# The trailing query product of each attention score taken over all 128 rows instead of 64

## The chip, the cores and the metric

The kernel runs on one core of one Trainium2 chip. The metric is the device time of one execution in microseconds (us); the median of three executions stands for the kernel.

## What is computed

Two layers over 1024 tokens of width 1024, in float32: an RMSNorm, one input projection, three mixers side by side (pooling, spatial gate, attention), an output projection onto the residual stream, then a second RMSNorm and a squared-ReLU MLP of width 4096. The change touches the attention, which has 8 heads of width 64 and no softmax: the weight of a key is its own sigmoid times the product of what all keys between it and the query left over.

```python
def stick_breaking_attention(q, k, v):
    ...
        z = jnp.einsum('bhqd,bhkd->bhqk', qi, k).astype(jnp.float32) * inv_sqrt_d
        ...
        log_beta = jax.nn.log_sigmoid(z)
        log_1m = jnp.where(causal, jax.nn.log_sigmoid(-z), 0.0)
        after = lax.cumsum(log_1m, axis=3, reverse=True) - log_1m
        a = jnp.where(causal, jnp.exp(log_beta + after), 0.0)
        return jnp.einsum('bhqk,bhkd->bhqd', a.astype(v.dtype), v)
```

## The kernel before

Features lie on the 128 partitions and tokens, in reversed order, on the free axis, in two chunks c of 512. Every large product runs as three single-pass products of operands that are split exactly into a leading and a trailing part of type float32r (`mm3`, L187 to L197). The tiles `xh`, `xl`, `wh`, `wl` are such parts of x and of a weight tile, and `pj` is the PSUM bank of an input projection.

A layer's attention goes through four head pairs `pr`, and each pair through 8 units: four pairs of query blocks (`c`, `j`) for each head `h` of the pair. A unit calls `sticks` twice, once per query block, and then `attend` of the unit before it (L527 to L537). Between units stand steps of projections: values, the next pair's k and q, pooling and gate (`fill`, L514 to L525). The last head pair has the first projections of the other mixers between its units.

`sticks` (L344) makes the score `z` of 128 queries with up to 512 keys in two products that accumulate into one bank:

- L354 multiplies `qh` by `kx`. A `kx` tile holds the leading part of one head's keys on 64 partitions and the trailing part on the other 64; a `qh` tile holds the leading part of q twice. One product over 128 rows therefore gives q-leading times all of k.
- L355 multiplies `ql`, the trailing part of q, by the leading part of k, over the 64 rows `HI[h]` alone (partitions 0 to 63 for head 0, 64 to 127 for head 1).

Then ScalarE makes two sigmoids `s` and `a` of z (L359, L360), GpSimd masks the diagonal block (L363), VectorE scans `s` to running products (L370), and GpSimd multiplies (L368, L373). `attend` transposes the weights `a` on TensorE (L391), ScalarE and VectorE split them into `th` and `tl` (L395, L397), TensorE multiplies both by the values into the one bank `av` (L401, L402), and L407 and L408 take that bank out to `y`.

`q_evac` (L316) makes `qh` and `ql` from a finished projection. Both heads of a pair share one `ql` tile of which each fills 64 rows; there are two such tiles, one per token chunk. ScalarE writes `qh` (L322), GpSimd its copy (L323), and VectorE `ql` (L326).

The order of the instructions is not written out by hand: the Tile framework traces the program and its scheduler orders each engine's queue by a timeline of its own (`schedule_with_timeline_sim`), helped by priorities (`early`) for the splits and evacuations. Each queue then runs strictly in the order given.

`add_sq` (L122) sums squares for the RMSNorm. At the very start, where x comes from memory, two engines keep a sum each: GpSimd in a tile of tag `rbc`, VectorE in a tile of tag `th`. The tag `rbc` also holds the inverse RMS laid out along the free axis (`bcast`, L160), and has three buffers.

Of the kernel before, what the change touches and what calls it, by code (L numbers as in the profile page):

```python
# [7 lines left out]
F32 = mybir.dt.float32  # L8
F32R = mybir.dt.float32r
# [16 lines left out]
NBIG = 4  # L26
# Pairs of query and key blocks of a unit, by its query blocks.
BLK = (15, 11, 7, 3)

# Units of attention are ordered by head pair, query blocks and head. Each product ahead of  # L30
# its use is traced between two units; from unit PACED on it follows their scores.
POOL_STEPS = 8
# [3 lines left out]
EVAC_EARLY = 400  # L36
# The last down projection by (chunk, first token, tokens), so that the final norm overlaps it.
TAIL = ((1, 0, 512), (0, 0, 256), (0, 256, 256))
# [8 lines left out]

# Column layout of the small constant array.
C_N1 = 0
# [7 lines left out]
def trunk_kernel(tc, xT, w_in, w_out, w_up, w_down, pool_w, sgw, sgb, sgn, cst, outT):  # L57
    """Decoder trunk with features on partitions and time, reversed, on the free axis.

    Every large product runs as three single-pass products of operands that are  # L60
    split exactly into a leading and a trailing part (float32r). The split of x
    carries the RMSNorm gain; the inverse RMS is applied to the products.
    """
    nc = tc.nc

    with ExitStack() as ctx:
# [44 lines left out]
        def put_x(k, c, src, gain):  # L111
            """Split src * gain (feature tile k, token chunk c) into xh + xl."""
            g = cs[:, gain + k : gain + k + 1]
            h = t512("xh", 16, F32R)
            nc.scalar.activation(h, src, AF.Copy, scale=g)
            lo = t512("xl", 16, F32R)
            nc.vector.scalar_tensor_tensor(
                out=lo, in0=src, scalar=g, in1=h.bitcast(F32), op0=ALU.mult, op1=ALU.subtract
            )
            xh[k, c], xl[k, c] = h, lo  # L120

        def add_sq(k, c, src, two=None):  # L122
            """Add the squares of src; two: a pool for a second sum, kept by another engine."""
            if k == 0:
                acc[c] = []
            new = len(acc[c]) <= int(two is not None)
            if new:
                acc[c].append(t512("th", 2, F32, two) if acc[c] else t512("rbc", 3))
            a = acc[c][k % len(acc[c])]
            sq = a if new else tmp()  # L130
            if two is None or k % 2:
                nc.scalar.activation(sq, src, AF.Square)
            else:
                nc.gpsimd.tensor_mul(sq, src, src)
            if not new:
                (nc.vector if two is not None and k % 2 else nc.gpsimd).tensor_add(a, a, sq)

        def rms_col(c):
            """Inverse RMS of chunk c, per token on partitions: rst[c][:, block]."""
            rst[c] = inv_rms([[a[:, b * P : (b + 1) * P] for a in acc[c]] for b in range(4)])  # L140
# [15 lines left out]
        def rms_row(c):  # L156
            """The same along the free axis, on all partitions: rbc[c]."""
            rbc[c] = bcast(rst[c], 4)

        def bcast(r, n):  # L160
            pb = psm()
            for b in range(n):
                nc.tensor.matmul(pb[:, b * P : (b + 1) * P], r[:, b : b + 1].broadcast_to([P, P]), ident, start=True, stop=True)
            bc = t512("rbc", 3)
            nc.scalar.copy(bc[:, 0 : n * P], pb[:, 0 : n * P])
            return bc
# [7 lines left out]
        def load_w(src, pool=None, tag="w", bufs=2):  # L174
            """Load a [128, 1024] weight tile and split it."""
            raw = per.tile([P, D], F32, tag="raw", name=nm("raw"), bufs=2)
# [10 lines left out]
        def mm3(ps, wx, first, last):  # L187
            """Accumulate the three products of each ((wh, wl), (xh, xl)) pair into ps."""
            n = len(wx)
# [9 lines left out]
        def proj(w, c, bank=None):  # L199
            """[128 features, 512 tokens] of x @ W for one column tile of W."""  # L200
            ps = (bank or psj)()
            mm3(
                ps,
                [((w[0][:, k * P : (k + 1) * P], w[1][:, k * P : (k + 1) * P]), (xh[k, c], xl[k, c])) for k in range(KT)],
                True, True,
            )
            return ps

        def proj_tok(w2, c, o, out):
            """[128 tokens, 256 features] of x @ W; w2 holds two halves of the rows of W."""  # L210
            for k in range(KT):
# [4 lines left out]
        def tok_steps(w2, start, evac):  # L216
            """One step per token block; two blocks share a bank."""
            bank = []
# [33 lines left out]
        def next_w(ahead=True):  # L252
            """The next weight tile in the order of use; ahead: also start on the one after it."""
            if not ready:
# [9 lines left out]
        for l in range(DEPTH):  # L264
# [3 lines left out]

# [1 line left out]
            arp = tc.tile_pool(name=f"ar{l}", bufs=1, side="right", reuse_waits="tile")  # L270
            ar = arp.__enter__()

            with (
# [8 lines left out]
                def v_steps(hf):  # L282
                    """Steps of the value projection of head pairs 2 hf and 2 hf + 1."""
                    w2 = []
# [31 lines left out]
                def q_evac(pr, c, ps):  # L316
                    t = tmp()
                    nc.vector.tensor_mul(t, ps, rbc[c])
                    qlo = t512("ql", 2, F32R, at)
                    for h in range(2):  # L320
# [3 lines left out]
                            out=qt[LO[h]], in0=t[HI[h]], scalar1=1.0, scalar2=0.0, op0=ALU.mult, op1=ALU.add  # L324
                        )
                        nc.vector.tensor_sub(qlo[HI[h]], t[HI[h]], qt[HI[h]].bitcast(F32))  # L326
                        qh[pr, h, c] = qt
                    ql[pr, c] = qlo

# [14 lines left out]
                def sticks(pr, h, i):  # L344
                    """Attention weights of query block i: {chunk of keys: [128 queries, 512 keys]}."""
                    c, o = divmod(i, 4)
                    qs = slice(o * P, (o + 1) * P)
                    prev, res = None, {}
                    for kc in ((0, 1) if c == 0 else (1,)):
# [4 lines left out]
                        nc.tensor.matmul(z[:, 0:w], qh[pr, h, c][:, qs], kt[:, lo:CH], start=True, stop=False)  # L354
                        mm = nc.tensor.matmul(z[:, 0:w], ql[pr, c][HI[h], qs], kt[HI[h], lo:CH], start=False, stop=True)  # L355
                        last_qk[0] = mm.ins.name
# [21 lines left out]
                def attend(pr, c, j, h, aw):  # L378
                    """Attention output of head h of a pair for query blocks 2 j and 2 j + 1."""
                    po = ap.tile([P, CH], F32, tag="av", name=nm("av"), bufs=1)  # L380
# [68 lines left out]
                def spread(steps, lo, hi):  # L449
                    """Trace the steps after the sticks of units lo to hi - 1, by their cost."""  # L450
                    cost = [BLK[units[n][2]] for n in range(lo, hi)]
# [17 lines left out]
                def pool_steps():  # L469
                    """Projection of the pooling mixer; its tiles take the place of used values."""  # L470
                    w = []
# [68 lines left out]

# [1 line left out]
            pop = tc.tile_pool(name=f"po{l}", bufs=1, space=PSUM, reuse_waits="tile")  # L542
# [54 lines left out]
            with tc.tile_pool(name=f"mx{l}", bufs=1, reuse_waits="tile") as mx:  # L597
# [3 lines left out]

                # pooling mixer
                pw = tmp()[:, 0:256].rearrange("p (i d) -> p i d", i=2)
# [43 lines left out]

                # spatial gate
                sw = tmp().rearrange("p (h t) -> p h t", h=4)
# [14 lines left out]
                def gelu(dst, src, t):  # L664
                    """dst = gelu(src), tanh form; src in SBUF."""
                    nc.gpsimd.tensor_mul(t, src, src)
# [51 lines left out]

                # output projection: the attention half of the width, then the rest
                split_y(1)  # L720
# [17 lines left out]

# [1 line left out]
            misc[0] = psg  # L740

            def finish(c, t, n, parts):
                """The final norm of tokens t to t + n - 1 of chunk c."""
                nb = n // P
# [72 lines left out]
def _layout(i):  # L817
# [7 lines left out]
    def mtiles(w):  # L825
        # [L, rows, cols] -> [L, cols/128, 128, rows]: one tile per 128 columns
        r, c = w.shape[1:]
        return w.reshape(L, r // P, P, c // P, P).transpose(0, 3, 2, 1, 4).reshape(L, c // P, P, r)

    def vtiles(w):  # L830
        # [L, 1024, cols] -> [L, cols/256 * 2, 128, 4 * 256]
        c = w.shape[2]
# [49 lines left out]
```

## Time and profile before

| | us |
|---|---|
| median of three executions | 2382.85 |
| lowest and highest | 2380.62, 2382.92 |
| span of the profiled execution | 2380.7 |
| granted TensorE clock, mean over that span | 0.983 |

The page gives the profiled execution's span alone. The three executions lie between 0.1 us under that span and 2.2 us over it, so next to nothing lies around it. The attention of the first layer lies in the first fifth of the span, from about 41 to 368 us, and that of the second from about 1222 to 1535 us. PE is the TensorE's matmuls and PEld its weight loads, which run beside them; DVE is VectorE, ACT ScalarE, POOL GpSimd. A row of a timeline starts with the instruction's start, then its duration. Matmuls are pipelined, so each row of a matmul overlaps the next one, and what a matmul occupies of the engine is the distance from its start to the start of the next.

### The profile page before, as it was taken

To read this page: it belongs to the slowest core of one execution; us is meant where nothing else is said; L and a number is where in the kernel's file an instruction comes from. 1 tells how busy PE (TensorE), PEld (TensorE's weight loads), DVE (VectorE), ACT (ScalarE), POOL (GpSimd) and SP (SyncE) were. 2 spreads that over 40 slices of the span, in tenths; PEclk is the share of its full clock that TensorE was granted. 3 is DMA by queue.
4 is the path that set the end of the run, shared out by engine and by line. 5 is a ranking of instruction groups with operands and counts; after the bars stand their busy time and mean duration, and the time that the engine had idled before them with its cause. 6 is when DMAs were issued, how large, how long until landed. Compare 5 with 4: busy or idle time off the path is not lost.

```text
span 2380.7 us, 28532 instructions
## 1 busy us (share of the span) xinstructions
PE 2333.8 (98%) x11224; PEld 1924.1 (81%) x11224; DVE 1264.0 (53%) x1606; ACT 728.8 (31%) x1321; POOL 803.3 (34%) x857
## 2 busy tenths in 40 slices
PE   8999999999999999999999999999999999999997
PEld 6887787788888888888887887878888888888887
DVE  7777668853432342342558777697433433432334
ACT  5556453430120120120445655534210210120121
POOL 6567575430110110110346757464110110110115
PEclk8999999999999999999999998999999999999998
DMA  3000102221220220220301010131211210220211
GB/s 125 27 28 28 33 10 89 67 62 31 67 62 18 62 71 9 62 71 18 120 23 36 19 40 28 32 98 45 71 35 37 71 45 30 68 62 18 62 36 71
DMA packets 40246, 118.40 MB, mean 50 GB/s; under 512 B 5040, under 2 KB 7600, under 8 KB 40112
## 3 DMA queue, kind: packets, MB, share of 16 engines
q1 hardware_dynamic: 38448, 114.48, 15.6%
q8 instruction: 88, 1.44, 0.3%
q10 hardware_dynamic: 1664, 2.10, 0.2%
q14 instruction: 46, 0.38, 0.0%
HBM read 108.17 MB, written 8.39 MB: 49 GB/s over the span
## 4 chain that ended last, share of the span: by engine, by line
PE 88%; DVE 6%; issue 3%; POOL 2%; ACT 1%; DMA 0%; DVEq 0%; SPq 0%; POOLq 0%; ACTq 0%
PE pj L191 14%; PE pj L196 14%; PE pj L197 14%; PE po L197 11%; PE po L196 11%; PE po L191 11%; PE z L355 3%; PE t L391 2%; PE z L354 2%; PE av L402 2%; PE av L401 1%; DVE s L370 1%; DVE yl L109 1%; DVE kx L691 1%; DVE xh L758 1%
## 5 line engine op out<-in xcount | busy, mean ns | idle before, releaser
L779 POOL TENSOR_TENSOR tmp<-tmp 128x512 f32<-128x512 f32 x128 | 177.6, 1387 | 1125.2 <-ACT ah L778 1118.0
L191 PE MATMUL pj<-xh,wh 128*128 128x512 f32 x1344 | 527.5, 392 | 0.0
L197 PE MATMUL pj<-xh,wl 128*128 128x512 f32 x1344 | 525.5, 391 | 0.0
L196 PE MATMUL pj<-xl,wh 128*128 128x512 f32 x1344 | 525.0, 391 | 0.0
L191 PE MATMUL po<-ah,dh 128*128 128x512 f32 (+1 forms) x1056 | 402.3, 383 | 2.3 <-DVE xa L798 2.3
L197 PE MATMUL po<-ah,dl 128*128 128x512 f32 (+1 forms) x1056 | 402.4, 384 | 0.0
L196 PE MATMUL po<-al,dh 128*128 128x512 f32 (+1 forms) x1056 | 402.2, 383 | 0.0
L798 DVE TENSOR_TENSOR xa<-po,xa 128x512 f32<-128x512 f32 (+1 forms) x264 | 177.9, 675 | 413.3 <-PE po L197 413.1
L778 ACT ACTIVATE ah<-tmp 128x512 fp32r<-128x512 f32 x128 | 80.4, 628 | 727.1 <-DVE tmp L774 727.1
L191 PEld LDWEIGHTS pj<-xh,wh 128*128 128x128 f32 x1344 | 252.4, 188 | 54.4 <-issue 3.2
L197 PEld LDWEIGHTS pj<-xh,wl 128*128 128x128 f32 x1344 | 252.3, 188 | 53.4 <-issue 1.7
L196 PEld LDWEIGHTS pj<-xl,wh 128*128 128x128 f32 x1344 | 252.5, 188 | 52.9 <-issue 1.6
L191 PEld LDWEIGHTS po<-ah,dh 128*128 128x128 f32 x1056 | 199.2, 189 | 41.2 <-DVE xa L798 2.5
L373 POOL TENSOR_TENSOR a<-a,s 128x255 f32<-128x255 f32 (+1 forms) x192 | 223.4, 1166 | 26.0 <-DVE s L370 13.6
L196 PEld LDWEIGHTS po<-al,dh 128*128 128x128 f32 x1056 | 199.3, 189 | 38.8
L197 PEld LDWEIGHTS po<-ah,dl 128*128 128x128 f32 x1056 | 199.2, 189 | 38.7
L774 DVE SCALAR_TENSOR_TENSOR tmp<-pj,rbc 128x512 f32<-128x512 f32 x124 | 85.5, 690 | 206.4 <-PE pj L197 196.5
L108 ACT CAST wh<-raw 128x1024 fp32r<-128x1024 f32 x116 | 121.6, 1048 | 198.9 <-PE pj L196 139.5
L109 DVE TENSOR_TENSOR wl<-raw,wh 128x1024 fp32r<-128x1024 f32 x116 | 154.5, 1332 | 33.8 <-ACT wh L108 32.9
L781 DVE TENSOR_TENSOR al<-tmp,ah 128x512 fp32r<-128x512 f32 x128 | 90.1, 705 | 146.2 <-POOL tmp L779 146.2
L370 DVE TENSOR_TENSOR_SCAN s<-s 128x256 f32<-128x256 f32 (+3 forms) x128 | 128.8, 1012 | 44.2 <-POOL s L363 41.7
L108 ACT CAST dh<-raw 128x1024 fp32r<-128x1024 f32 x64 | 67.2, 1049 | 207.7 <-DMA raw<-in_w_down 207.7
(165 smaller groups left out, 3552.0 us busy)
## 6 DMA issues: line engine op xcount, KB each, us to landing
raw<-in_w_up SPq DMA_DIRECT2D x64, 512.0 KB, 3.6
raw<-in_w_down SPq DMA_DIRECT2D x64, 512.0 KB, 3.6
raw<-in_w_in SPq DMA_DIRECT2D x36, 512.0 KB, 3.6
raw<-in_w_out SPq DMA_DIRECT2D x16, 512.0 KB, 3.6
tmp<-in_xT SPq DMA_DIRECT2D x16, 256.0 KB, 2.7
xd<-xa SPq DMA_DIRECT2D x16, 256.0 KB, 2.0
tmp<-xd SPq DMA_DIRECT2D x16, 256.0 KB, 2.7
a<-in_xT SPq DMA_DIRECT2D x12, 256.0 KB, 5.3
```

Of the source, the lines that this page charges most:

```text
L108: nc.scalar.copy(hi, src)
L109: nc.vector.tensor_sub(lo, src, hi.bitcast(F32))
L191: mm = nc.tensor.matmul(ps, ah, bh, start=first and i == 0, stop=False)
L196: nc.tensor.matmul(ps, ah, bl, start=False, stop=False)
L197: nc.tensor.matmul(ps, al, bh, start=False, stop=last and i == n - 1)
L370: nc.vector.tensor_tensor_scan(sl, sl, sl, 1.0 if prev is None else prev[:, CH - 1 : CH], ALU.mult, ALU.bypass)
L373: nc.gpsimd.tensor_mul(a[:, lo + 1 : CH], a[:, lo + 1 : CH], s[:, lo : CH - 1])
L774: nc.vector.scalar_tensor_tensor(out=r, in0=ps, scalar=0.0, in1=rbc[c], op0=ALU.max, op1=ALU.mult)
L778: nc.scalar.activation(h, r, AF.Square)
L779: nc.gpsimd.tensor_mul(r, r, r)
L781: nc.vector.tensor_sub(lo, r, h.bitcast(F32))
L798: nc.vector.tensor_add(x, ps, x)
```

## The change

L355 runs over all 128 rows. For that each head gets a `ql` tile of its own (tags `ql0`, `ql1`, two buffers each), whose 64 rows `LO[h]` GpSimd sets to zero each time a tile is made: 32 new instructions, four for each head pair and layer. The zero rows meet the trailing part of k, so the score stays the same. To make room the tag `rbc` loses one of its three buffers, and the GpSimd sum at the start moves from an `rbc` tile to a tile of tag `tl` in the attention's pool. Comments are taken out too, which moves later lines by two.

```diff
         def add_sq(k, c, src, two=None):
...
-                acc[c].append(t512("th", 2, F32, two) if acc[c] else t512("rbc", 3))
+                acc[c].append(t512("rbc", 2) if two is None else t512("th" if acc[c] else "tl", 2, F32, two))
...
-            bc = t512("rbc", 3)
+            bc = t512("rbc", 2)
...
                 def q_evac(pr, c, ps):
                     t = tmp()
                     nc.vector.tensor_mul(t, ps, rbc[c])
-                    qlo = t512("ql", 2, F32R, at)
                     for h in range(2):
                         qt = t512("qh", 4, F32R, at)
                         nc.scalar.copy(qt[HI[h]], t[HI[h]])
...
+                        qlo = t512(f"ql{h}", 2, F32R, at)
+                        nc.gpsimd.memset(qlo[LO[h]].bitcast(F32), 0.0)
                         nc.vector.tensor_sub(qlo[HI[h]], t[HI[h]], qt[HI[h]].bitcast(F32))
-                        qh[pr, h, c] = qt
-                    ql[pr, c] = qlo
+                        qh[pr, h, c], ql[pr, h, c] = qt, qlo
...
-                        mm = nc.tensor.matmul(z[:, 0:w], ql[pr, c][HI[h], qs], kt[HI[h], lo:CH], start=False, stop=True)
+                        mm = nc.tensor.matmul(z[:, 0:w], ql[pr, h, c][:, qs], kt[:, lo:CH], start=False, stop=True)
```

No instruction but the 32 memsets is added or taken away on any compute engine. The scheduler however makes a somewhat different order of the same work in the attention of both layers. Two places follow; the numbers in the names are the program's own and differ between the two kernels.

VectorE, first layer, where the last head pair begins (`s` are scans, `tl` the trailing parts of the transposed weights, `pa` the pooling projection). Before:

```order
L326 TENSOR_TENSOR ql_3093<-tmp_3091,qh_3098 64x512
L370 SCALAR_TENSOR_TENSOR s_2991<-s_2991 128x384
L370 SCALAR_TENSOR_TENSOR s_3138<-s_3138 128x256
L370 SCALAR_TENSOR_TENSOR s_3004<-s_3004,s_2991 128x512
L397 TENSOR_TENSOR tl_2855<-t_2848,th_2853 128x512
L397 TENSOR_TENSOR tl_3018<-t_3012,th_3016 128x384
```

The same place in the changed kernel:

```order
L481 TENSOR_TENSOR pa_3132<-pj_3133,rbc_269 128x512
L372 SCALAR_TENSOR_TENSOR s_3012<-s_3012 128x384
L372 SCALAR_TENSOR_TENSOR s_3162<-s_3162 128x256
L399 TENSOR_TENSOR tl_2873<-t_2866,th_2871 128x512
L372 SCALAR_TENSOR_TENSOR s_3025<-s_3025,s_3012 128x512
L399 TENSOR_TENSOR tl_3039<-t_3033,th_3037 128x384
```

The 512-wide `tl` has moved ahead of the 512-wide scan that stood before it; the order of TensorE's rows around it is the same in both.

GpSimd, a little earlier in the same layer, in the last units of the third head pair (`a` and `s` are the attention weights and sticks, `qh` the copy of q for the fourth pair, the memset of `tmp` belongs to the pooling mixer). Before:

```order
L363 AFFINE_SELECT s_2802<-s_2802 128x128
L373 TENSOR_TENSOR a_2793<-a_2793,s_2792 128x511
L604 MEMSET tmp_4139 128x256
L323 TENSOR_SCALAR qh_3094<-tmp_3091 64x512
L651 AFFINE_SELECT tmp_4207<-tmp_4207 128x512
L363 AFFINE_SELECT a_2803<-a_2803 128x128
L373 TENSOR_TENSOR a_2803<-a_2803,s_2802 128x383
```

The same place in the changed kernel:

```order
L365 AFFINE_SELECT s_2820<-s_2820 128x128
L375 TENSOR_TENSOR a_2811<-a_2811,s_2810 128x511
L328 MEMSET ql_647_3117 64x512
L365 AFFINE_SELECT a_2821<-a_2821 128x128
L375 TENSOR_TENSOR a_2821<-a_2821,s_2820 128x383
L370 TENSOR_TENSOR a_2834<-a_2834,s_2820 128x1
L375 TENSOR_TENSOR a_2834<-a_2834,s_2833 128x511
L606 MEMSET tmp_4163 128x256
```

A memset of a `ql` tile now stands between a mask and the next products, and the other mixers' preparations come later. The first four memsets of the first layer stand at the head of GpSimd's queue, behind the memset of the identity matrix and ahead of the first squares; those of the second layer stand behind the last sums of squares and ahead of the inverse RMS.

## Rows read from the trace of the kernel before

**Rows 1.** The page: busy time, share of span and instructions of each engine.

```profile
PE 2333.8 (98%) x11224; PEld 1924.1 (81%) x11224; DVE 1264.0 (53%) x1606; ACT 728.8 (31%) x1321; POOL 803.3 (34%) x857
```

**Rows 2.** The page: the chain that ended last, shares of the span by engine.

```profile
PE 88%; DVE 6%; issue 3%; POOL 2%; ACT 1%; DMA 0%; DVEq 0%; SPq 0%; POOLq 0%; ACTq 0%
```

**Rows 3.** Windows, last two head pairs, layer 0: length, busy PE, PEld, DVE, ACT, POOL, PEclk.

```profile
194.00:276.00 82.00, 80.58 (x420) 63.10 (x419) 62.09 (x79) 45.92 (x98) 50.05 (x72) 1.00 0.13 40
276.00:342.00 66.00, 60.66 (x321) 48.67 (x321) 45.94 (x57) 35.62 (x81) 47.69 (x67) 0.84 0.04 13
```

**Rows 4.** Line L355: durations in ns, and the count of each shape.

```profile
L355 PE MATMUL z<-kx,ql x192: 222/490/793, 41.2 to 1508.2; 64*128 64x512 f32 x96, 64*128 64x256 f32 x32, 64*128 64x128 f32 x32, 64*128 64x384 f32 x32
```

**Rows 5.** Timeline of PE's matmuls, 300 to 312 us: start, duration, line, rows*columns, shape.

```profile
300.74 0.28 PE L354 MATMUL z<-kx,qh 128*128 128x256 f32 x1
300.95 0.38 PE L355 MATMUL z<-kx,ql 64*128 64x256 f32 x1
301.26 0.38 PE L402 MATMUL av<-tl,v 128*128 128x256 f32 x1
...
302.90 0.50 PE L354 MATMUL z<-kx,qh 128*128 128x512 f32 x1
303.34 0.49 PE L355 MATMUL z<-kx,ql 64*128 64x512 f32 x1
303.76 0.39 PE L401 MATMUL av<-th,v 128*128 128x256 f32 x1
303.98 0.22 PE L354 MATMUL z<-kx,qh 128*128 128x128 f32 x1
304.13 0.33 PE L355 MATMUL z<-kx,ql 64*128 64x128 f32 x1
304.39 0.50 PE L354 MATMUL z<-kx,qh 128*128 128x512 f32 x1
...
305.70 0.28 PE L191 MATMUL pj<-wh,xh 128*128 128x256 f32 x1
305.82 0.29 PE L196 MATMUL pj<-wl,xh 128*128 128x256 f32 x1
```

**Rows 6.** Timeline, 150 to 175 us: another score, and ordinary 512-column products.

```profile
153.88 0.40 PE L197 MATMUL pj<-xh,wl 128*128 128x512 f32 x1
153.88 0.19 PEld L191 LDWEIGHTS pj<-xh,wh 128*128 128x128 f32 x1
...
154.11 0.39 PE L191 MATMUL pj<-xh,wh 128*128 128x512 f32 x1
...
161.12 0.40 PE L354 MATMUL z<-kx,qh 128*128 128x512 f32 x1
161.44 0.18 PEld L355 LDWEIGHTS z<-kx,ql 64*128 64x128 f32 x1 [0.25 <-issue]
161.44 0.49 PE L355 MATMUL z<-kx,ql 64*128 64x512 f32 x1
...
161.87 0.39 PE L196 MATMUL pj<-wl,xh 128*128 128x256 f32 x1
```

**Rows 7.** Timeline, 268 to 284 us: the longest wait of PE in that attention.

```profile
279.18 1.95 DVE L370 TENSOR_TENSOR_SCAN s<-s,s 128x512 f32<-128x512 f32 x1
...
281.06 1.12 DVE L397 TENSOR_TENSOR tl<-t,th 128x512 fp32r<-128x512 f32 x2
...
281.77 0.58 PE L402 MATMUL av<-tl,v 128*128 128x256 f32 x1 [2.91 <-DVE tl L397]
```

**Rows 8.** Timeline of POOL at the start.

```profile
0.78 0.21 POOL masks.py:197 MEMSET ident<- 128x128 f32 x1 [0.29 <-POOLq L872]
...
4.36 1.04 POOL L134 TENSOR_TENSOR rbc<-a 128x512 f32<-128x512 f32 x1 [3.00 <-DMA a<-in_xT]
```

**Rows 9.** Timeline of POOL at the turn of the layers.

```profile
1206.49 2.00 POOL L153 TENSOR_TENSOR rst<-rst,mhalf 128x4 f32<-128x4 f32 x2 [13.72 <-DVE rst L149]
```

**Rows 10.** Groups by shape: the copies of q on POOL.

```profile
L323 POOL TENSOR_SCALAR qh<-tmp 64x512 fp32r<-64x512 f32 x32 | 30.6, 956 | 20.7 <-DVE tmp L318 10.6 <-issue 6.6 <-PE z L354 1.5
```

## The prediction

> **What bounds the kernel now.** I read the page first, then the chain, then the windows by head pair, then the timeline of TensorE (PE) around a few scores. The page shows PE busy for 98% of the span, and no other engine above 53% [rows 1]; the chain that ended last lies on PE for 88% of its length [rows 2]. A microsecond saved on PE is therefore worth something nearly everywhere, if the others keep up. The windows tell where they might not. In the third head pair PE is busy for 80.58 of 82 us, and VectorE (DVE), the next engine, for 62.09. In the fourth PE is busy for only 60.66 of 66 us, and its mean granted clock is 0.84 [rows 3]. With two levels, 1.2 and 2.4 GHz, a mean of 0.84 over 66 us means some 21 us at 1.2 GHz. The reader should see two different stretches: in one everything waits for PE, and I take the first two head pairs to be like it; in the other PE waits for others too.
>
> **What a score costs on PE.** What counts is the distance from one matmul's start to the next. An ordinary product of 512 columns takes 153.88 to 154.11 = 0.23 us, and one of 256 columns 305.70 to 305.82 = 0.12 [rows 5, 6]. A score of 512 columns is two products. In one of them the 128-row product starts at 302.90, the 64-row one at 303.34 and the next instruction at 303.76: 0.44 + 0.42 = 0.86 us [rows 5]. In another it is 161.12, 161.44, 161.87, so 0.32 + 0.43 = 0.75 [rows 6]. Two ordinary products would take 0.46. The weight loads show why: an ordinary load starts one product ahead (the load for the product at 154.11 starts at 153.88), but the load for the 64-row product starts at 161.44, in the same instant as its product, after 0.25 us in which nothing that the profile shows held it [rows 6]. Going into the 64-row product and coming out of it, a load of about 0.19 us stands uncovered. The way in shows as 0.32 to 0.44 us and the way out as 0.42 to 0.43, instead of 0.23.
>
> **The main term: both products over 128 rows.** I take it that a 128-row product with half its weights zero runs like every other 128-row product, whose loads are covered. The saving for each score is what it takes now less two ordinary products:
> - 512 columns: 0.75 to 0.86 less 0.46 is 0.29 to 0.40; 96 of them [rows 4] give 28 to 38 us, middle 33.
> - 256 columns: 300.74 to 300.95 to 301.26 is 0.52, less 0.24 is 0.28; 32 give 9 us [rows 4, 5].
> - 384 columns: no row here; between the two above I take 0.31, 32 give 10 us (9 to 13).
> - 128 columns: 303.98, 304.13, 304.39 is 0.41; an ordinary one is no longer than one of 256 columns, so at least 0.41 less 0.24 = 0.17; 32 give 5.5 us [rows 4, 5].
>
> The sum is 58 us, with bounds of 51 and 65. The trace does not show a 128-row product with zero rows; the bound from the other side is that nothing is saved (a rival below). I take the full value, because all other 128-row products of the trace, whatever they hold, run at the ordinary distance.
>
> The Trainium skill has a rule that speaks against this term. Its page "TensorE: Matmul & The Clock Gate", section "Why this matters for your kernels", says that a single matmul over few rows takes as long as one over 128, and that the gain of few rows lies only in running several at once. Taken alone it would make the sum zero, since the columns stay the same. The trace agrees for the load itself but not for the distance between starts, 0.42 against 0.23 us [rows 5, 6].
>
> **What is given back.** The 58 us leave PE, but the chain of a score through ScalarE, GpSimd (POOL) and DVE is as long as before. The four head pairs of the two layers hold equal numbers of scores, so each of the eight takes 7.25 us of the saving.
> - Three quarters, 43.5 us: a third head pair would take 82 - 7.25 = 74.75 us, and DVE's 62.09 us would fill 83% of it, POOL's 50.05 us 67% [rows 3]. That leaves room but more collisions; I take a return of one eighth, 5 us (0 to 20).
> - The last head pair of both layers, 14.5 us: PE already idles 5.3 us of 66 there [rows 3]. A PE that comes earlier to the same waits only waits longer. I take two thirds back, 9.5 us (0 to 14.5).
> - The longest wait there, 2.91 us for DVE's `tl`, stands behind a scan of 1.95 us on DVE [rows 7]. In the new order that `tl` comes before the scan, so the wait loses up to 1.95 us, if the same happens in both layers 4 us; I take 2, as the scan feeds work that is wanted soon after.
>
> **The memsets.** 32 on POOL. Their price is not in the trace; the nearest rows are a memset of 128 columns, 0.21 us [rows 8], and POOL's copy of 64x512, 0.956 us [rows 10]. That is 7 to 31 us on an engine that is idle for two thirds of the span; nearer by shape is the copy, by kind the memset, and I take 0.7 each, 22 us. The first four lie in the 3.00 us in which POOL waits for the first x [rows 8]; the next such four in the 13.72 us before the inverse RMS of the second layer [rows 9]. The other 24 stand in the queue between masks and products of the attention. In a head pair four of them, 2.8 us (up to 3.8), raise POOL's share of the third pair's shortened 74.75 us from 67 to 71%. A memset waits for the last use of its tile by PE, and the masks of the next units are queued behind it, which the scans on DVE want. I cost it at nothing on the path, as the cover is POOL's own idle time; if that cover is gone, each costs its 0.2 to 1 us, at most 24 us in all.
>
> **The smaller buffers.** `rbc` with two buffers holds the two chunks' rows; at the turn to the MLP and at the final norm a third would be wanted only while the first is still read, and its readers are done a projection earlier. The sum moved to `tl` changes no engine. I cost both at zero.
>
> **The sum.** 2380.7 - 58 + 5 + 9.5 - 2 = 2335.2 us of span. The three executions lie 0.1 under to 2.2 over the span, so I add 1: **2336 us**, 2.0% faster. For this case alone the bounds of the saving and of the returns give 2318 to 2354.
>
> **The rivals.**
> - *The clock recovers too.* The 21 us at 1.2 GHz in the last head pair cost up to 10 us of work, in each layer [rows 3]. If the shorter waits and denser products keep the clock up, up to 20 us come on top: 2336 - 20 = 2316, and with smaller returns as little as 2300; I put it at 2312. For it: the reordered `tl`. Against it: PE comes earlier to every other wait.
> - *The attention is bound by its chains.* If DVE's and POOL's queues, contending with each other, can't run at 83% and 71%, two thirds of the saving turn into waits: 2380.7 - 19 = 2362. For it: the fourth head pair as it is now; against: PE idles 1.4 us in all of the third.
> - *The rows don't matter.* The uncovered loads come from something else, such as the two products' shared bank or operands, and stay: 2381 to 2384, no change. Against it: the projections also add product after product to one bank, at 0.23 us.
> - *Slower: waits that take the clock down.* A wait like that of 2.91 us [rows 7] ends in a stretch with 21 us at 1.2 GHz [rows 3]; if half of that belongs to it, it loses 5 us of work besides, and such an event costs about 8 us. The saving of 58 us is eaten by seven of them, and from the eighth on the kernel is slower; with nine it takes 2380.7 - 58 + 72 = 2395. For it: a fuller DVE, and a memset on POOL that waits for PE ahead of the masks. Against: the third head pair, with more projection steps between its units, keeps a granted clock of 1.00 [rows 3].
>
> **How the numbers follow.** The forecast has 0.64, the better clock 0.12, bound chains 0.13, no change 0.04, slower 0.07. Faster by over 0.2% (about what a measurement of this kernel can tell from no change) is the first three together, 0.89; within 0.2% is 0.04; slower by over 0.2% is 0.07. The range reaches over the forecast's own, over half of the better clock down to 2308 and over half of the bound chains up to 2364.
>
> **What would show it.** In the profile after, the weight load of the second score product starts ahead of its product, and the distances at both score lines are 0.23 us at 512 columns; that decides the main term. The windows of the first three head pairs are each 6 to 7 us shorter with PE still busy throughout: right for the first return. In the fourth, PE idles longer than 5.3 us and the stretch is shortened by 2 to 4 us: right for the second. New waits of PE for `tl` or for a scan's product, and a granted clock under 0.84, would make the prediction too low; a distance of 0.42 that stays would make it wrong altogether.

## The result and the profile after

The changed kernel takes **2353.2 us** (median; executions from 2352.5 to 2358.1) against 2382.75 for the kernel before in the same comparison: a recorded ratio of 0.9886, 95% interval 0.9872 to 0.9900 (the two medians by themselves give 0.9876), so 29.6 us or 1.2% faster. The forecast was 2336 us with a range of 2308 to 2364. The sign and the main mechanism were right; some 17 us of the expected gain are missing, and the runs below are about where they went.

The page of the changed kernel, engine busy times and the chain that ended last, answering to [rows 1, 2]:

```profile
PE 2268.2 (96%) x11224; PEld 1917.9 (82%) x11224; DVE 1264.1 (54%) x1606; ACT 725.5 (31%) x1321; POOL 824.4 (35%) x889
...
PE 79%; DVE 9%; POOL 6%; issue 3%; ACT 2%; DMA 0%; SPq 0%; POOLq 0%; DVEq 0%; ACTq 0%
```

PE is busy 65.6 us less, yet the span is only 28.8 us shorter (2380.7 to 2351.9). The other 37 us are new idle time of PE, and nine hundredths of the chain have passed from PE to VectorE, GpSimd and ScalarE.

The second product of the score, all shapes, answering to [rows 4], and two scores on PE at 290 us, answering to [rows 5], with the weight load that belongs to the first of the rows (start, duration, line, rows*columns, shape):

```profile
L357 PEld LDWEIGHTS z<-kx,ql x192: 186/191/338, 43.4 to 1480.6; 128*128 128x128 f32 x192
L357 PE MATMUL z<-kx,ql x192: 222/391/629, 43.5 to 1480.8; 128*128 128x512 f32 x96, 128*128 128x256 f32 x32, 128*128 128x128 f32 x32, 128*128 128x384 f32 x32
```

```profile
289.78 0.19 PEld L357 LDWEIGHTS z<-kx,ql 128*128 128x128 f32 x1
...
290.01 0.39 PE L357 MATMUL z<-kx,ql 128*128 128x512 f32 x1
...
290.24 0.28 PE L403 MATMUL av<-th,v 128*128 128x256 f32 x1
...
290.53 0.45 PE L356 MATMUL z<-kx,qh 128*128 128x512 f32 x1
290.81 0.39 PE L357 MATMUL z<-kx,ql 128*128 128x512 f32 x1
291.05 0.28 PE L191 MATMUL pj<-wh,xh 128*128 128x256 f32 x1
```

The way out of the second product is now 290.24 - 290.01 = 0.23 and 291.05 - 290.81 = 0.24 us, where it was 0.42 to 0.43; the way in is 0.28 here and 0.236 in the median of the 512-column scores, though a quarter of them still take over 0.31. The weight load takes 0.19 us as before, but it starts 0.23 us ahead of its product (289.78 to 290.01), beside other work. Before, 131 of the 192 loads of this line stood behind 33.6 us of idle time that the profile puts down to "issue"; now none does.

The first layer's four head pairs, before and after (length of the stretch, then busy us of PE, PEld, DVE, ACT and POOL with their counts, and the granted clock; [rows 3] showed two of these stretches, cut a little differently). Before:

```profile
41.20:120.00 78.80, 77.83 (x422) 63.03 (x422) 58.97 (x77) 42.89 (x97) 50.56 (x68) 0.91 0.09 28
120.00:194.60 74.60, 74.60 (x443) 61.35 (x442) 58.32 (x77) 44.08 (x98) 49.99 (x68) 1.00 0.08 22
194.60:275.70 81.10, 79.68 (x416) 62.40 (x414) 61.29 (x79) 45.02 (x96) 49.15 (x71) 1.00 0.14 41
275.70:367.70 92.00, 86.66 (x517) 73.42 (x516) 58.35 (x73) 46.51 (x100) 54.07 (x71) 0.89 0.08 24
```

After:

```profile
43.50:115.10 71.60, 66.99 (x432) 60.75 (x432) 56.95 (x73) 43.00 (x98) 48.57 (x66) 0.98 0.10 30
115.10:185.70 70.60, 66.26 (x423) 59.32 (x422) 59.66 (x80) 41.72 (x94) 51.51 (x73) 0.98 0.08 24
185.70:263.70 78.00, 74.66 (x426) 65.85 (x425) 60.85 (x79) 46.02 (x99) 52.04 (x75) 0.96 0.14 42
263.70:352.00 88.30, 77.36 (x517) 70.77 (x516) 57.81 (x72) 45.50 (x99) 56.52 (x75) 0.90 0.07 22
```

The stretches are shorter by 7.2, 4.0, 3.1 and 3.7 us, and PE's idle time in them, the length less its busy time, has gone from 1.0, 0.0, 1.4 and 5.3 us to 4.6, 4.3, 3.3 and 10.9. In the second layer they are shorter by 4.4, 1.5, 2.3 and 1.9. The first stretch owes a good part of its 7.2 to a clock that went from 0.91 to 0.98.

PE's longest waits after, by what it waited for (us in total, times, longest):

```profile
PE av L404 <- DVE tl L399: 12.5, 11, 4.1
PE t L393 <- DVE tl L399: 9.4, 5, 3.8
PE av L403 <- DVE y L410: 8.9, 8, 1.9
...
PE pj L191 <- DVE v L300: 6.6, 4, 3.9
PE z L356 <- ACT a L362: 5.6, 8, 1.9
```

Before, the first of these groups held 5.2 us in three waits, the third 3.4 in two. What PE waits for in these groups is mostly VectorE's output.

### The profile page after: what moved, and what is told of

It reads as the page before. It is cut to its first block, busy times and chain, and to the rows that moved or that the text cites. A ratio compares the mean times of both kernels' runs of the same rounds, so it can differ in the third digit from the quotient of the medians.

```text
span 2351.9 us, 28573 instructions
## 1 busy us (share of the span) xinstructions
PE 2268.2 (96%) x11224; PEld 1917.9 (82%) x11224; DVE 1264.1 (54%) x1606; ACT 725.5 (31%) x1321; POOL 824.4 (35%) x889
## 4 chain that ended last, share of the span: by engine, by line
PE 79%; DVE 9%; POOL 6%; issue 3%; ACT 2%; DMA 0%; SPq 0%; POOLq 0%; DVEq 0%; ACTq 0%
PE pj L191 13%; PE pj L196 13%; PE pj L197 13%; PE po L197 12%; PE po L196 12%; PE po L191 11%; DVE s L372 3%; POOL a L375 2%; PE t L393 2%; PE av L403 1%; PE av L404 1%; POOL s L365 1%; POOL a L365 1%; PE z L356 1%; PE z L357 1%
```

## Experiments

Times are medians; "the changed kernel" is 2353.2 us. Each edit is to the changed kernel. The kernel before, measured beside each of them, took 2379.5 to 2382.7 us, so a difference of under some 3 us between two kernels of this section says nothing.

### The same order with 64 rows

```diff
-mm = nc.tensor.matmul(z[:, 0:w], ql[pr, h, c][:, qs], kt[:, lo:CH], start=False, stop=True)
+mm = nc.tensor.matmul(z[:, 0:w], ql[pr, h, c][HI[h], qs], kt[HI[h], lo:CH], start=False, stop=True)
```

The scheduler gives every engine the same order, row for row, so this pair differs in the rows of 192 products alone.

> The changed kernel with its second score product back on 64 rows; tiles, memsets and the order of every engine's queue are those of the changed kernel, row for row. Theory A (the saving of about 60 us on TensorE is real, and half of it comes back because TensorE reaches the ends of VectorE's and GpSimd's chains earlier): the waits of TensorE fall to about 13 us in the attention as before, the distances return to 0.42 us, and the time is that of the kernel before, 2378 to 2386 us. Theory B (half comes back because the new order and the memsets cost some 30 us by themselves, whatever TensorE does): 2353 + 60 = 2405 to 2415 us.

Measured: 2376.45 us, ratio to before 0.9977 (0.9967 to 0.9987). So tiles, memsets and new order together are worth 6 us even with the old product, and the rows alone are worth 2376.45 - 2353.2 = 23.2 us. Both layers' attention, with 64 rows and then with 128:

```profile
43.70:362.70 319.00, 311.40 (x1793) 255.29 (x1793) 237.21 (x301) 178.22 (x387) 205.81 (x285) 0.97 0.10 28
1216.90:1529.70 312.80, 305.30 (x1737) 248.78 (x1737) 230.31 (x296) 174.17 (x380) 205.06 (x283) 0.97 0.10 28
```

```profile
43.50:352.10 308.60, 285.37 (x1793) 256.78 (x1793) 235.37 (x301) 176.24 (x387) 208.63 (x286) 0.95 0.10 29
1206.10:1508.70 302.60, 279.05 (x1738) 250.89 (x1737) 229.38 (x297) 172.65 (x380) 210.42 (x283) 0.95 0.10 29
```

The attention is 20.6 us shorter in sum. PE's idle time in it rises from 15.1 to 46.8 us, 31.7 more. The mean clock falls from 0.97 to 0.95: of 632 us that is a loss of some 19 us, of 611 us one of some 31, so 12 more. The last digit of the clock makes this uncertain by some 6 us; PE's busy time in the stretches with a granted clock of 1.2 GHz, 32 us with 64 rows and 52 with 128, gives 10. So 20.6 + 31.7 + 10 to 12 = 62 to 64 us is the gross saving on PE, an estimate, of which two thirds came back as waits and as time at 1.2 GHz. VectorE's work is the same in both.

One place shows how. It is the start of the first layer's last head pair, that of [rows 7]. With 64 rows:

```profile
272.83 0.94 POOL L322 TENSOR_SCALAR qh<-tmp 64x512 fp32r<-64x512 f32 x1
...
274.42 0.29 POOL L365 TENSOR_SCALAR_AFFINE_SELECT s<-s 128x128 f32<-128x128 f32 x1
...
274.74 1.83 DVE L372 TENSOR_TENSOR_SCAN s<-s 128x384 f32<-128x384 f32 x2 [0.73 <-POOL s L365]
...
275.97 0.38 PE L403 MATMUL av<-th,v 128*128 128x256 f32 x1
276.49 0.67 DVE L399 TENSOR_TENSOR tl<-t,th 128x512 fp32r<-128x512 f32 x1
...
277.21 0.38 PE L404 MATMUL av<-tl,v 128*128 128x256 f32 x1 [0.86 <-DVE tl L399]
```

With 128 rows:

```profile
265.61 0.28 PE L403 MATMUL av<-th,v 128*128 128x256 f32 x1
265.69 0.61 POOL L322 TENSOR_SCALAR qh<-tmp 64x512 fp32r<-64x512 f32 x1
...
266.36 0.52 POOL L328 MEMSET ql<- 64x512 f32 x1
266.95 0.29 POOL L365 TENSOR_SCALAR_AFFINE_SELECT s<-s 128x128 f32<-128x128 f32 x1
...
267.28 1.83 DVE L372 TENSOR_TENSOR_SCAN s<-s 128x384 f32<-128x384 f32 x2 [2.25 <-POOL s L365]
...
269.02 0.67 DVE L399 TENSOR_TENSOR tl<-t,th 128x512 fp32r<-128x512 f32 x1
...
269.74 0.58 PE L404 MATMUL av<-tl,v 128*128 128x256 f32 x1 [3.86 <-DVE tl L399]
```

PE comes to the wait 10.4 us earlier (275.97 to 265.61), VectorE's `tl` only 7.5 us earlier (276.49 to 269.02), and so the wait grows by 3.0 us, from 0.86 to 3.86. `tl` is late since it stands behind two scans, these wait for a mask, and the mask stands behind the copy of q and the memset on GpSimd, which has no gap there.

### Half of every scan left out, with 128 and with 64 rows

```diff
-sl = s[:, lo:CH]
+sl = s[:, lo : lo + w // 2]
```

> The changed kernel with every scan over the first half of its keys alone; the second half of the sticks stays as the sigmoid left it, so this part of the computation is left out. About 100 us of VectorE's work go, 50 in each layer's attention; TensorE's work stays. Theory A (half of the saving comes back because TensorE now waits for VectorE's queue): TensorE's waits in the attention fall from 47 us to under 15, the clock's low stretches with them, and the time is 2353 - 30 to 45 = 2308 to 2323 us. Rival C (the waits come from the length of the chain or from GpSimd and ScalarE, not from VectorE's load): less than 12 us faster, 2341 us or more.

Measured: 2297.56 us, ratio 0.9652 (0.9637 to 0.9666): 55.6 us less than the changed kernel, more than any theory had. The waits of PE nearly vanish and the clock stays up:

```profile
46.50:328.40 281.90, 272.58 (x1793) 245.93 (x1793) 190.35 (x301) 175.50 (x387) 178.63 (x286) 1.00 0.11 32
1182.50:1454.30 271.80, 265.07 (x1739) 239.33 (x1738) 183.74 (x297) 171.70 (x380) 174.79 (x283) 1.00 0.11 32
```

PE is idle for 16 us here instead of 46.8. By itself that shows only that scans are dear when PE is fast. The second kernel therefore has the same half scans, the same order row for row, and the product back at 64 rows (the edit of the 64-row run above).

> This kernel is the one in which half of every scan is left out (2297.56 us), in the same order of instructions, with the second product of the score back at 64 rows; like that one it leaves half of the running products uncomputed, and its time is read against that one alone. Theory A (the saving of about 60 us is whole on TensorE, and VectorE's chain of scans and splits gave back the part that is missing in the changed kernel): with VectorE relieved the rows are worth nearly all of it, 50 to 62 us, so 2348 to 2360 us, with TensorE idle no longer in the attention than with 128 rows by more than a few us. Theory R (the rows themselves are worth only the 23 us measured between the two kernels of one order, whatever VectorE does): 2316 to 2326 us.

Measured: 2350.17 us, 52.6 us more than with 128 rows. Its four executions lie between 2347.3 and 2358.3 us, so this difference is known to some 5 us, and the profile is that of the longest. Its attention:

```profile
46.40:354.70 308.30, 306.97 (x1792) 251.62 (x1792) 190.92 (x301) 177.67 (x387) 174.74 (x286) 0.99 0.10 29
1210.80:1513.40 302.60, 301.62 (x1737) 246.34 (x1737) 182.10 (x297) 174.16 (x380) 171.46 (x283) 0.98 0.10 29
```

This settles the main question. With the full scans the rows are worth 23.2 us, with half of them 52.6, each pair in one order of its own; the theory that the rows are worth only 23 falls. Read the other way round, halving the scans is worth 26.3 us with 64 rows (2376.45 to 2350.17) and 55.6 with 128, the change of order included. The scheduler ordered the half-scan kernels differently from the changed one, so a part of the 29 us between 23.2 and 52.6 may be the order's; how much is not shown. The saving on PE was there all the time, and the chain through the scans took back most of what is missing.

That chain is not VectorE's alone. GpSimd's work is the same in the changed kernel and in the one with half scans, but its 569 instructions in the attention take 353 us there instead of 419. One of its groups over the whole kernel, the changed one first:

```profile
L370 POOL TENSOR_TENSOR a<-a,s 128x1 f32<-128x1 f32 x64 | 45.1, 705 | 11.1 <-ACT a L362 10.6
```

```profile
L370 POOL TENSOR_TENSOR a<-a,s 128x1 f32<-128x1 f32 x64 | 18.5, 290 | 7.0 <-ACT a L362 6.9
```

A product of a single column takes 0.705 us in the mean beside full scans and 0.290 beside half ones: most of it is standing still (the last section shows behind what). So the runs don't tell VectorE's own load from what its scans cost GpSimd.

### The price of the zero rows

A second memset of each tile, and, in another kernel, the zero rows written by ScalarE:

```diff
+nc.gpsimd.memset(qlo[LO[h]].bitcast(F32), 0.0)
```

```diff
-nc.gpsimd.memset(qlo[LO[h]].bitcast(F32), 0.0)
+nc.scalar.activation(qlo[LO[h]], t[HI[h]], AF.Copy, scale=0.0)
```

> The changed kernel with each memset of the zero rows made twice, 64 memsets of about 0.5 us in place of 32 (the scheduler reorders a little for it). Theory M (the memsets in GpSimd's queue hold up the masks and with them the scans): 8 to 20 us slower than the changed kernel, 2361 to 2373 us. Theory A (GpSimd has the room): within 3 us of it, 2350 to 2356 us.

> The changed kernel with the zero rows written by ScalarE (a copy with scale 0) in place of GpSimd's memset, so that GpSimd has none of the added work. Theory M: 5 to 15 us faster than the changed kernel, 2338 to 2348 us. Theory A: the same within 4 us, since VectorE is what TensorE waits for.

Measured: 2342.76 us (0.9837, 0.9821 to 0.9854) with 32 memsets more, 2350.08 (0.9866) with none on GpSimd. The first misses both theories: more work made the kernel 10.4 us faster. The edit changes the scheduler's order, and the gain lies in one layer: the second layer's attention takes 289.9 us instead of 302.6, the first layer's 309.5 instead of 308.6. A memset takes 0.52 us, 16.4 us of GpSimd's time for all 32. What they cost the kernel can't be told apart from the order: with none on GpSimd it is 3 us faster, with 32 more it is 10 us faster.

### Where PE's new waits are ended

Five kernels go at the waits. The first gives two units' outputs the two halves of one bank, so that the next unit need not wait until `y` has been taken out of it:

```diff
-po = ap.tile([P, CH], F32, tag="av", name=nm("av"), bufs=1)
+if not avb:
+    bank = ap.tile([P, CH], F32, tag="av", name=nm("av"), bufs=1)
+    avb.extend((bank[:, 256:512], bank[:, 0:256]))
+po = avb.pop()
```

> The changed kernel, in the same order of every queue, with the attention output of two units in turn in the two halves of one bank, so that only every second unit's first av product waits for the evacuation of the unit before. Theory P (the single av bank holds TensorE: 8.9 us of its waits are for y): 4 to 9 us faster, 2344 to 2349 us. Theory A (VectorE's queue is late as a whole): the wait goes over to tl, which comes out of the same queue, and the time stays within 2 us of 2353.

Measured: 2353.24 us (0.988, 0.9866 to 0.9895), unchanged, with the `y` waits still 8.9 us in 8 times. The edit did not take the wait away, so it says nothing on what the wait is worth.

The second raises the priority of `th`, `tl` and `y`:

```diff
-th = t512("th", 2, F32R, at)
...
+with early(400):
...
+    nc.vector.tensor_sub(tl[:, 0:wd], pt[:, 0:wd], th[:, 0:wd].bitcast(F32))
```

> The changed kernel with the split of the transposed weights (th, tl) and the evacuation of the attention output given a higher priority in the scheduler. The work is the same; the order is the same in the first layer and differs in some 150 rows of TensorE and 47 of VectorE in the second layer's attention. Rival O (the order that the scheduler happens to make is worth up to 10 us, now that TensorE has little slack): the second layer's attention differs by over 3 us either way while the first stays within 1.5 us. Theory A alone, with nothing in the order: the whole time within 2 us of 2353.

Measured: 2350.91 us (0.9873, 0.9859 to 0.9888). The first layer keeps its order, the second is 2.5 us shorter. The total of the waits for `tl` stays (14.0 and 6.3 us instead of 12.5 and 9.4), and that for `y`, which was raised too, grows from 8.9 to 11.9: bringing one VectorE instruction forward puts another back.

The third keeps 16 instead of 8 of the pooling projection's steps for the last head pair, as other work for PE:

```diff
-POOL_STEPS = 8
+POOL_STEPS = 16
```

> The changed kernel with all 16 projection steps of the other mixers spread over units 22 to 31, in place of 8 there and 8 behind the attention. The same work, but TensorE has something to do while the last head pair's chains run. Theory A: TensorE's idle time in the last head pair, 11 us in each layer, falls under 4, the low clock there goes, and the time is 12 to 30 us less than the changed kernel's, 2323 to 2341 us. Rival C (VectorE and GpSimd set the pace there whatever TensorE does, and the evacuations of the added steps load VectorE further): within 5 us of 2353.

Measured: 2347.88 us (0.9862, 0.9847 to 0.9877), 5.3 us less. The first layer's last head pair:

```profile
272.60:352.00 79.40, 76.64 (x527) 70.05 (x526) 58.45 (x70) 43.42 (x95) 50.62 (x66) 1.00 0.10 34
```

Its idle time falls from 10.9 to 2.8 us and its clock rises from 0.90 to 1.00. The third pair, which ends with more of the steps, is longer by as much (87.0 us instead of 78.0), so that the two together take the time that they took, with PE busy for 160 us of them instead of 152. Of these 8 us part is lost again behind the attention: in the stretch after the attention, PE idles 12.4 us instead of 6.5 in the first layer and 24.2 instead of 18.8 in the second (to the end of the span), mostly waiting for parts of `y` that the output projection now wants sooner.

The fourth moves the subtraction that makes `ql` from VectorE to GpSimd, and a fifth that of `kx` as well:

```diff
-nc.vector.tensor_sub(qlo[HI[h]], t[HI[h]], qt[HI[h]].bitcast(F32))
+nc.gpsimd.tensor_sub(qlo[HI[h]], t[HI[h]], qt[HI[h]].bitcast(F32))
```

```diff
-nc.vector.tensor_sub(kt[LO[h]], t[HI[h]], kt[HI[h]].bitcast(F32))
+nc.gpsimd.tensor_sub(kt[LO[h]], t[HI[h]], kt[HI[h]].bitcast(F32))
```

> The changed kernel with the subtraction that makes ql on GpSimd in place of VectorE: 32 instructions, about 28 us off VectorE and about 30 onto GpSimd, over both layers. Theory A (VectorE's queue): 4 to 12 us faster, 2341 to 2349 us. Rival M (GpSimd is as short of room as VectorE): 0 to 15 us slower, 2353 to 2368 us.

> The changed kernel with two subtractions of the attention on GpSimd instead of VectorE, that for ql (alone 2346.1 us, 7 us less than the changed kernel) and that for the trailing half of kx; nothing else differs, and the last head pair keeps its eight pooling steps. It takes some 12 us more per layer from VectorE and gives GpSimd as much, which then is as busy in the attention as VectorE. Theory A (what VectorE is spared comes back on TensorE, at the rate of ql_pool, 7 us for 18 us spared in both layers): another 4 to 9 us, 2337 to 2342 us. Theory G (GpSimd, which masks the scans' input and multiplies their output, is by then as much a bound as VectorE): 2346 to 2358 us.

Measured: 2346.11 us (0.9857, 0.9841 to 0.9874), 7.1 us less, with the first; 2352.66 (0.9882, 0.9865 to 0.9898), as much as the changed kernel, with both. The sums over both layers' attention, for the first and for both:

```profile
sum 602.10, PE 557.92 PEld 500.54 DVE 446.41 ACT 345.67 POOL 449.99; mean PE 278.96 PEld 250.27 DVE 223.20 ACT 172.83 POOL 224.99
```

```profile
sum 603.90, PE 556.80 PEld 499.02 DVE 424.80 ACT 346.08 POOL 484.28; mean PE 278.40 PEld 249.51 DVE 212.40 ACT 173.04 POOL 242.14
```

From VectorE 18 us went away, then 40 (it had 464.75); to GpSimd came 31, then 65 (419.06), as a 64x512 subtraction takes 1.4 to 1.6 us there and 0.8 to 0.9 on VectorE. The first step gains, the second gives its gain back: by then GpSimd, at 80% of the attention, is the fuller of the two. That fits a chain which both engines hold, but does not show it: 7 us is no more than a new order alone is worth here.

### Gains put together

The `ql` subtraction on GpSimd with 12 pooling steps, and the same with the zero rows by ScalarE.

> The changed kernel with two edits that each gained alone or may gain: the subtraction that makes ql on GpSimd instead of VectorE (alone 2346.1 us), and twelve instead of eight pooling projection steps kept for the last head pair (sixteen alone: 2347.9 us). Theory A (VectorE's load and the thin filling of the last head pair give back separate parts): the gains add, 2336 to 2344 us. Theory O (each gain is mostly the scheduler's order, which falls anew with every edit): anywhere from 2342 to 2358 us.

> The same two edits and, third, the zero rows of ql written by ScalarE instead of GpSimd (alone 2350.1 us), so that GpSimd's queue has 32 instructions less. Theory A (separate parts add): 2333 to 2342 us. Theory O (order falls anew): 2342 to 2358 us.

Measured: 2358.88 us (0.9909, 0.9894 to 0.9924) and 2371.71 (0.9966, 0.9953 to 0.9979). The first gave 7 us alone, the third 3, and 16 steps gave 5 (12 steps were not run alone); the two kernels are 6 and 18 us slower than the changed kernel. In the last, PE is busy for 592 us of the attention instead of 564, with the steps that were brought in, and still idles there for 46 us, as long as in the changed kernel: the attention is 26 us longer, and the stretches behind it, which gave up those steps, are only 9 us shorter, since PE idles 10 us more in them. The gains don't add, and why these orders fill PE's waits so badly wasn't settled. The fastest kernel that computes the whole remains the one with the second memset, 2342.76 us, by the luck of its order.

## Why the prediction was right, and which of its terms was not

- **The main term held.** 58 us were predicted (51 to 65). The two kernels of one order give 62 to 64; with half scans, 57.2 us of length (610.9 to 553.7) and 13.7 of added idle time, less some 9 for a clock that rose to 1.00, give 62. The weight load starts ahead and the distance fell from 0.42 to 0.23 us, as the step said. The rule of the Trainium skill that the prediction weighed, page "TensorE: Matmul & The Clock Gate", section "Why this matters for your kernels", says that a single matmul over few rows takes as long as one over 128. The trace agrees as far as the loads go (0.183 us in the median with 64 rows, 0.191 with 128), but not for the distance between starts in a stream of other products.
- **The return was the mis-sized term.** 14.5 us were put down, 5 of them for the first three head pairs of each layer and 9.5 for the last, and 2 as a gain at one wait. Measured in one order, 41 to 43 came back of 62 to 64. By head pair, with the prediction's 7.25 us for each and against the kernel before, the first three pairs gave back 43.5 - 22.5 = 21 us (7.2, 4.0, 3.1 and 4.4, 1.5, 2.3 saved), over the bound of 20, and the last 14.5 - 5.6 = 9. These savings have the gain of the new order in them. In one order the pairs saved 5.2, 1.1, 3.0 and 1.1 us in the first layer and 4.6, 1.1, 3.6 and 0.9 in the second, so the first three gave back 25 us and the last 12.5, more than the 9.5 put down but within its bound. Most of the miss lies in the first three pairs. The step that failed is "that leaves room but more collisions; I take a return of one eighth": a DVE share of 83% was read as spare time, but it is on a chain in which ScalarE, GpSimd and VectorE wait for each other in turn, and PE no longer hid those turns.
- **The order had a gain that the sum did not have.** With 64 rows the new order is already 6 us faster; the prediction allowed 2 us, for the `tl` moved ahead of a scan. At that place it was right on the order, as the wait of 2.91 us is 0.86 there with 64 rows. The rows then took it back: with 128 it is 3.86. The 6 us themselves go with the granted clock: with 64 rows the first layer's first pair has 0.98 instead of 0.91, the last pairs 0.92 instead of 0.89, and PE is busy at 1.2 GHz for 32 us of the attention instead of 54, which is worth 11 us; against that it idles 2 us more there and starts 2.5 us later. Nobody chose the order for its clock, so this part of the result is luck.
- **The memsets** took 0.52 us each where 0.7 was taken. That they cost nothing on the path is not shown: the kernel without them on GpSimd is 3 us faster, but in another order. **The start**, where the sum moved to `tl` stands, was put at nothing and was not free: the first score starts at 43.5 us instead of 41.2. Whether the moved sum or the new order did it is not shown; where some of it lies is. Four subtractions for `xl` start at some 23 us on VectorE in both kernels. Before, they fall into the 5.81 us in which GpSimd waits; after, they run beside its squares and its sum. Before:

```profile
L117 DVE SCALAR_TENSOR_TENSOR xl<-s,cs,xh 128x512 fp32r<-128x512 f32 x4 | 2.7, 744 | 0.0
...
26.43 1.48 POOL L134 TENSOR_TENSOR tmp<-a 128x512 f32<-128x512 f32 x1 [5.81 <-DVE th L136]
```

After:

```profile
L117 DVE SCALAR_TENSOR_TENSOR xl<-s,cs,xh 128x512 fp32r<-128x512 f32 x4 | 4.5, 1191 | 0.0
...
23.25 1.49 POOL L134 TENSOR_TENSOR tmp<-a 128x512 f32<-128x512 f32 x1 [2.56 <-DVE th L136]
24.70 1.71 POOL L136 TENSOR_TENSOR tl<-tl,tmp 128x512 f32<-128x512 f32 x1
```

- **The rivals.** "Bound by its chains", at 2362, is what happened for the rows by themselves: it let two thirds of the saving turn into waits, and 41 to 43 of 62 to 64 us did. It lacked the order's gain; with that the result lies between the two, 9 us under it and 17 over the forecast. "The clock recovers too" fell: the last head pair has 0.90 after 0.89, and in one order it sinks from 0.92 to 0.90 with the denser waits. "Slower" had its mechanism in part, more waits and with them a lower clock, at a price of some 10 to 12 us of clock and not of 72. "The rows don't matter" is ruled out by both pairs.
- In sums: -58 + 14.5 - 2 was predicted; about -63 + 42 for the rows, and -7.5 in the span for the order, is what the traces show. The bounds that the prediction gives "for this case alone", 2318 to 2354, don't come out of its own terms: with 51 to 65 saved, 0 to 20 and 0 to 14.5 returned and the 2 and the 1 us as they stand, the sum runs from about 2315 to 2363.

## What to carry to other kernels

A product over fewer rows than its neighbours can cost more than one over all rows, where it stands alone among them: look at the distances between starts and at whether its weight load begins ahead. Where PE hides a chain that runs through three other engines, a busy share of 80% on one of them is not room; size the return by the place where PE already waits, since the others can come to be like it once PE is faster (in the first layer 3.3 to 4.6 us idle in each, where the fourth had 5.3 before). And where a scheduler makes the order, one edit's time holds some 10 us of order besides, so compare kernels of one order, and change the suspected load in both of them.

## What the runs showed of the hardware

- VectorE and GpSimd hold each other up by more than I had taken in. GpSimd's product of one column takes 0.705 us in the mean beside full scans and 0.290 beside half ones, and VectorE's `xl` 1.191 instead of 0.744 beside a GpSimd sum, while the memset, which reads nothing, takes 0.52 us in every kernel that has it. The changed kernel's trace tells which VectorE instructions do it. Of its 64 products of one column, 40 start beside one with both inputs in SBUF, where the tiles lie; they take 0.64 to 1.20 us and end within 0.06 us of that one's end. Another 19 start beside one with an input in PSUM, where the matmuls' banks `t`, `av` and `pj` lie, and take 0.18 to 0.20, as do the 5 beside an idle VectorE. One of each kind:

```profile
170.78 0.67 DVE L399 TENSOR_TENSOR tl<-t,th 128x512 fp32r<-128x512 f32 x1
...
171.21 0.19 POOL L370 TENSOR_TENSOR a<-a,s 128x1 f32<-128x1 f32 x1 [0.76 <-ACT a L362]
```

```profile
231.34 1.86 DVE L372 TENSOR_TENSOR_SCAN s<-s,s 128x512 f32<-128x512 f32 x1
...
232.07 1.11 POOL L370 TENSOR_TENSOR a<-a,s 128x1 f32<-128x1 f32 x1
```

  By the page "SBUF — State Buffer" of the Trainium skill, section "SBUF: two separate sides", a VectorE instruction with two SBUF inputs and a GpSimd one that reads SBUF take turns at a shared pair of ports, one for its whole length. The trace agrees with that, the untouched memset too; no run here changes the inputs alone.
- PE's waits and its clock go together: 31.7 us more of idle time came with a mean clock of 0.95 instead of 0.97, and where the idle time went, with half scans or in the last head pair with more filling, the granted clock was 1.00.
